# Gated DeltaNet gates with the tokens on the partitions, and an input norm with the token loads first, scaled on VectorE alone

## The chip, the cores and the metric

The kernel runs on one core of one Trainium2 chip. A core has five engines that run side by side and meet only at semaphores: TensorE (PE, matrix products and transposes into PSUM; its weight loads are listed apart as PEld), VectorE (DVE), ScalarE (ACT, activation functions and copies), GpSimd (POOL) and SyncE (SP), which here issues the transfers. Sixteen DMA engines move the data. The metric is the device time of one execution in microseconds, lower is better, given as the median of the runs.

## The reference

One inference step of a two-layer trunk: layer 0 is a gated DeltaNet mixer, layer 1 an RWKV-7 mixer, each behind an RMSNorm and with a residual add. The input is 16 meta tokens and 1024 prompt tokens of one sequence, and 8 sequences of 8 sample tokens with states of their own. The change lies at the start of layer 0:

```
xn = rmsnorm(x, norm_w[0])                      # per token, 1024 features
proj = xn @ w_in                                # qkv (4096), z (2048), b (16), a (16)
qkv = silu(causal_conv(qkv))                    # 4 taps
beta = sigmoid(b)                               # per token and value head
g = -exp(a_log) * softplus(a + dt_bias)         # log decay, per token and value head
gc = cumsum(g) within a chunk
decay = exp(gc[i] - gc[j]), i >= j
A = I + strictly lower (beta k k^T * decay)     # inverted per chunk
```

There are 16 value heads and 8 key heads; value heads 2j and 2j+1 share key head j. Everything behind the gates uses gc in three forms: exp(gc) and exp(gc_last - gc) per token, exp(gc_last) per chunk, and the matrix of differences.

## The kernel before

**Layout.** The 1104 tokens (64 sample tokens, 16 meta tokens, 1024 prompt tokens) are nine tiles of up to 128. Tile 0 holds the 64 sample tokens (eight blocks of 8), the meta tokens and the first 48 prompt tokens. For the products the tokens are the free axis in three segments of 384, 384 and 336, and the features are the partitions. FP32 values are split into a rounded high part and a low rest, and each product of a 128-feature block is three matmuls (high x high, low x high, high x low), so a product of 128 outputs over one segment is 24 matmuls.

**The norm** (`input_norm`, lines 280 to 314) works tile by tile with tokens on the partitions, in the groups {0,1}, {2,3,4}, {5,6}, {7,8}: ACT squares and sums, POOL raises to the power -1/2, DVE refines by a Newton step (lines 111 to 113). Tiles 0, 1, 2, 4, 6 and 8 are then scaled by one DVE instruction (line 299); tiles 3, 5 and 7 are multiplied by the norm weights on POOL (line 291) and scaled on ACT (line 301). PE turns each tile by eight transposes (line 74), ACT copies the high parts (line 309) and DVE subtracts for the low parts (line 313).

**The gates** (`gates_open`, `gates`) have the 16 heads on 16 partitions and all 1104 tokens on the free axis. The product with the 32 gate columns of w_in is `d` with 64 output rows. ACT and DVE work on 16 partitions (lines 361 to 371), one scan makes gc (line 373), and differences to the chunk's last gc are formed by DVE (lines 379 to 382). The decays of the chunks' ends go through memory to all partitions (`dgl` to `eglb`), gc goes to memory as `drow`, and nine transposes turn gates to tokens on partitions, `gcol`, whose four columns are beta, -gc, exp(gc) and exp(gc_last - gc).

**What sets the order.** Up to the first product of layer 0 a planner, which simulates the program, orders every engine. From there on PE and ACT follow a written order: `gdn_events` puts work at slots u, where a slot is half a product over one segment (12 matmuls) and slot -24 is the first half of key head 0's keys. `product` makes the keys (`dk`), queries (`dq`), values (`dv`) and gates (`dz`) of a head in turn; each segment's result is copied by ACT to `raw`, convolved (`cvy`: one tap on ACT, three on DVE, line 524), and passed through SiLU. DVE, POOL and SP still follow the planner.

The gates' stages stand at slots -22.9, -19.4, -16.8, -16.7 and -16.6 (line 928). The pair decays of head 0 (`decays`, line 643: load `E` from `drow`, POOL select, ACT exponentials) are loaded at -18.5, and their exponentials stand from -16 on. Then come the scores (`fsc`, -15.2 to -13.6), the decayed matrix (line 710), its way through memory (`ltd`) to `invA`, and the inversion of 32x32 blocks in 31 steps of two DVE instructions (lines 571 and 573). A transposing copy (line 741) and more transfers (`g_t`, `T1n`) end it, and the first merge of blocks on PE (`rY`, written at slot 2.5) uses it. The attention decays (`attn`) are loaded in the same way; there are three loads of each kind for each of the eight key heads.

Of the kernel before, what the change touches and what calls it, by code (L numbers as in the profile page):

```python
# [11 lines left out]
ALU = mybir.AluOpType  # L12
# [24 lines left out]
class Builder:  # L37
# [242 lines left out]
    def input_norm(self, xh, xl):  # L280
        nc, i, t, lp = self.nc, self.i, self.t, self.lp
        for qs in [[0,1],[2,3,4],[5,6],[7,8]]:
# [3 lines left out]
            for u, q in enumerate(qs):  # L286
                x, nr = self.xrows[q]
                junk = t(lp, [128, D], "junk", 1, BF16)
                self.act(junk[0:nr], x[0:nr], AF.Square, accum=ss[0:nr, u:u + 1])
                if q not in (0,1,2,4,6,8):  # L290
                    nc.gpsimd.tensor_tensor(x[0:nr], x[0:nr], self.nwb[0:nr], op=ALU.mult)
# [3 lines left out]
            for u, q in enumerate(qs):  # L295
                x, nr = self.xrows[q]
                r = rs[0:nr, u:u + 1]
                if q in (0,1,2,4,6,8):
                    nc.vector.scalar_tensor_tensor(x[0:nr], x[0:nr], r, self.nwb[0:nr], op0=ALU.mult, op1=ALU.mult)
                else:  # L300
                    self.act(x[0:nr], x[0:nr], AF.Identity, scale=r)
                c = 128 * q
                for h in (0, 1):
                    p = self.ps("f", 2) if h else self.ps("r", 3)
                    for k in range(4):
                        self.transpose(p[:, 128 * k:128 * k + nr], x[0:nr, 512 * h + 128 * k:512 * h + 128 * k + 128])
# [10 lines left out]
    def gates_open(self, ctx):  # L317
        nc, i = self.nc, self.i
        W = i["gdn_w_in"][0]

        self.col = self.t(self.l0, [128, 9, 4, 16], "gcol")
        self.eglb = self.t(self.l0, [128, 16, 17], "eglb")
        self.bmask4 = self.t(self.l0, [64, 4], "bmask4")
# [3 lines left out]
        t = self.t  # L327
        al = t(gp, [128, 2], "al")
# [5 lines left out]
        rows = t(gp, [96, 1152], "rows")  # L334
        nc.vector.memset(rows, 0.0)
        g = t(gp, [48, 1152], "g")
        nc.vector.memset(g[32:48], 0.0)
        sm = t(gp, [48, 1152], "sm")
        nc.vector.memset(sm[32:48], 1.0)
        nc.gpsimd.memset(sm[32:48].rearrange("p (c k) -> p c k", k=128)[:, :, 0:1], 0.0)  # L340
        nc.gpsimd.memset(sm[32:48, 0:72].rearrange("p (c k) -> p c k", k=8)[:, :, 0:1], 0.0)
        self.gate_in = al, wz, rows, g, sm
        nc.sync.dma_start(al[32:48, 0:1], i["gdn_a_log"].rearrange("l h -> h l"))
        nc.sync.dma_start(al[32:48, 1:2], i["gdn_dt_bias"].rearrange("l h -> h l"))

    def gates(self, xh, xl):
        nc, i, t, gp = self.nc, self.i, self.t, self.gatep
        al, wz, rows, g, sm = self.gate_in
        nea = t(gp, [128, 1], "nea")
        self.act(nea[32:48], al[32:48, 0:1], AF.Exp)  # L350
        nc.vector.tensor_scalar(nea[32:48], nea[32:48], -1.0, None, op0=ALU.mult)
# [4 lines left out]
        x = t(gp, [48, NT], "ax")  # L356
        y = t(gp, [48, NT], "ay")
        for s, (c0, n) in enumerate(SEGS):
            p = self.dense(w, 64, xh, xl, s)
            b = rows[0:16, c0:c0 + n]  # L360
            self.act(b, p[0:16, 0:n], AF.Tanh, scale=0.5)
            nc.vector.tensor_scalar(b, b, 0.5, 0.5, op0=ALU.mult, op1=ALU.add)
            xa, ya = x[32:48, c0:c0 + n], y[32:48, c0:c0 + n]
            self.act(xa, p[32:48, 0:n], AF.Identity, bias=al[32:48, 1:2])
            nc.vector.scalar_tensor_tensor(ya, xa, -1.0, xa, op0=ALU.mult, op1=ALU.max)
            self.act(ya, ya, AF.Exp, scale=-1.0)
        yield
        xa, ya = x[32:48], y[32:48]
        self.act(ya, ya, AF.Ln, bias=1.0)
        nc.vector.scalar_tensor_tensor(ya, xa, 0.0, ya, op0=ALU.max, op1=ALU.add)  # L370
        nc.vector.tensor_scalar(g[32:48, 0:NT], ya, nea[32:48], None, op0=ALU.mult)
        gc = rows[32:48]
        nc.vector.tensor_tensor_scan(gc, sm[32:48], g[32:48], 0.0, op0=ALU.mult, op1=ALU.add)
        yield
        gd = rows[64:80]
        c3 = lambda x: x.rearrange("p (c k) -> p c k", k=128)
        c8 = lambda x: x[:, 0:64].rearrange("p (c k) -> p c k", k=8)
        v, v8 = c3(gc), c8(gc)
        nc.vector.tensor_tensor(c3(gd)[:, 1:9], v[:, 1:9, 127:128].broadcast_to([16, 8, 128]), v[:, 1:9], op=ALU.subtract)
        nc.vector.tensor_tensor(c3(gd)[:, 0:1, 64:128], v[:, 0:1, 127:128].broadcast_to([16, 1, 64]), v[:, 0:1, 64:128],  # L380
                                op=ALU.subtract)
        nc.vector.tensor_tensor(c8(gd), v8[:, :, 7:8].broadcast_to([16, 8, 8]), v8, op=ALU.subtract)
        egl = t(gp, [48, 17], "egl")
        self.act(egl[32:48, 0:8].unsqueeze(2), v8[:, :, 7:8], AF.Exp)
        self.act(egl[32:48, 8:17].unsqueeze(2), v[:, :, 127:128], AF.Exp)
        dgl = self.dram([16, 17], "dgl")
        nc.sync.dma_start(dgl, egl[32:48])
        nc.sync.dma_start(self.eglb.rearrange("p h c -> p (h c)"),
                          dgl.rearrange("(o h) c -> o (h c)", o=1).broadcast_to([128, 272]))

# [530 lines left out]
    def gdn_events(self, G, open_, gate, swap):  # L921
# [6 lines left out]
        for u in (-22.9, -19.4, -16.8, -16.7, -16.6):  # L928
            self.at(u, gate)
# [1622 lines left out]
```

## Time and profile before

| what | value |
|---|---|
| median of 3 runs | 2184.01 us (2181.36 to 2190.6) |
| profiled execution, its own time | 2190.08 us |
| its span on the core | 2188.3 us |
| PE, DVE, ACT, POOL busy | 94%, 72%, 59%, 38% |
| mean granted PE clock | 0.981 |

A busy share is a mean over all stages. In a timeline each row is: start in us, length in us, engine, line, operation, written tile <- read tiles, shapes, how many instructions were merged into the row, and in brackets how long the engine stood before it and what ended that. A row that merges several has their sum as its length. A line can be that of a helper: line 74 is every transpose, line 77 every product, line 63 every activation.

### The profile page before, as it was taken

How to read it: one execution, taken by the hardware profiler on the slowest of the kernel's cores; microseconds unless marked ns; L12 is line 12 of the kernel's file. 1: busy time of each engine (PE TensorE's matmuls, PEld its weight loads, DVE VectorE, ACT ScalarE, POOL GpSimd, SP SyncE). 2: the span in 40 equal slices, each digit the busy share in tenths (PEclk: the TensorE clock that was granted, in tenths of full speed). 3: DMA queues.
4: the chain of work that ended last, by engine and by line, in shares of the span. 5: the costliest groups of instructions: out<-in, count | busy, mean ns of one | idle time of the engine just before them, and what ended most of it. 6: DMA issues, size and time to landing. Idle time of an engine off the chain costs nothing. (4 is left out here: it accounts for less than half of the span.)

```text
span 2188.3 us, 54818 instructions
## 1 busy us (share of the span) xinstructions
PE 2048.3 (94%) x20404; PEld 1905.8 (87%) x20404; DVE 1585.8 (72%) x4221; ACT 1290.9 (59%) x3761; POOL 841.2 (38%) x1125
## 2 busy tenths in 40 slices
PE   5869899999999999999999999999898999999997
PEld 5859899999999999998899999888898988888876
DVE  7967869788887979795334676757968657777755
ACT  5526466656565665656533365664746446777774
POOL 3423333334343333334231352343534344444444
PEclk9979999999999999999999999999999999999999
DMA  4423342424333333335345115655565476677764
GB/s 119 119 58 87 90 115 85 116 78 106 96 96 106 105 96 102 98 102 165 97 126 134 61 51 190 215 167 168 168 180 152 119 221 175 181 229 221 239 178 138
DMA packets 430661, 292.65 MB, mean 134 GB/s; under 512 B 147145, under 2 KB 412986, under 8 KB 430394
## 3 DMA queue, kind: packets, MB, share of 16 engines
q1 hardware_dynamic: 430394, 289.14, 46.0%
q8 instruction: 161, 2.64, 0.5%
q14 instruction: 106, 0.87, 0.1%
HBM read 197.68 MB, written 91.37 MB: 132 GB/s over the span
## 5 line engine op out<-in xcount | busy, mean ns | idle before, releaser
L91 POOL TENSOR_TENSOR wlo<-wraw,whi 128x512 fp32r<-128x512 f32 (+1 forms) x246 | 328.5, 1337 | 475.8 <-ACT whi L87 432.1
L77 PE MATMUL d<-xc,whi 128*128 128x384 f32 (+2 forms) x1006 | 279.1, 336 | 0.8 <-DVE xc L313 0.7
L524 DVE SCALAR_TENSOR_TENSOR cvy<-raw,cw,cvy 128x408 f32<-128x408 f32 (+2 forms) x288 | 189.1, 657 | 19.2 <-ACT cvy L63 17.8
L87 ACT CAST whi<-wraw 128x512 fp32r<-128x512 f32 (+1 forms) x246 | 149.9, 612 | 87.2 <-PE d L77 50.0
L77 PEld LDWEIGHTS d<-xc,whi 128*128 128x128 f32 (+1 forms) x1006 | 183.0, 189 | 3.4 <-DVE xc L313 1.1
L77 PE MATMUL d<-xc,wlo 128*128 128x384 f32 (+3 forms) x476 | 157.5, 339 | 3.8 <-POOL wlo L91 3.8
L77 PE MATMUL dz<-xc,whi 128*128 128x384 f32 (+1 forms) x480 | 153.7, 338 | 0.0
L77 PE MATMUL dv<-xc,whi 128*128 128x384 f32 (+1 forms) x480 | 152.2, 337 | 0.0
L77 PE MATMUL d<-xa,whi 128*128 128x384 f32 (+3 forms) x450 | 142.9, 341 | 8.4 <-ACT ev L2352 4.1
L63 ACT ACTIVATE o<-rA,gcol 128x128 f32<-128x128 f32 x128 | 42.2, 367 | 116.2 <-DVE S L903 116.0
L571 DVE TENSOR_TENSOR invtmp<-invA,invT 72x31 f32<-72x31 f32 (+15 forms) x248 | 101.8, 411 | 3.2
L77 PE MATMUL dv<-xa,whi 128*128 128x384 f32 (+1 forms) x288 | 99.0, 344 | 0.0
L77 PE MATMUL dz<-xa,whi 128*128 128x384 f32 (+1 forms) x288 | 98.5, 342 | 0.0
L77 PEld LDWEIGHTS d<-xc,wlo 128*128 128x128 f32 (+1 forms) x476 | 89.2, 189 | 7.9 <-POOL wlo L91 4.9
L77 PEld LDWEIGHTS d<-xa,whi 128*128 128x128 f32 (+1 forms) x450 | 84.3, 190 | 12.9 <-ACT ev L2352 4.4
L573 DVE TENSOR_TENSOR invT<-invT,invtmp 72x31 f32<-72x31 f32 (+15 forms) x248 | 92.7, 374 | 3.3
L77 PEld LDWEIGHTS dz<-xc,whi 128*128 128x128 f32 x480 | 89.3, 188 | 4.6 <-issue 4.5
L77 PEld LDWEIGHTS dv<-xc,whi 128*128 128x128 f32 x480 | 89.1, 188 | 1.4 <-issue 1.4
L77 PE MATMUL d<-xa,wlo 128*128 128x384 f32 (+3 forms) x252 | 84.8, 337 | 2.0 <-POOL wlo L91 2.0
L77 PE MATMUL dq<-xc,whi 128*128 128x384 f32 (+1 forms) x240 | 78.3, 343 | 3.0 <-ACT whi L87 3.0
L77 PE MATMUL dk<-xc,whi 128*128 128x384 f32 (+1 forms) x240 | 78.2, 346 | 0.0
L1333 DVE SCALAR_TENSOR_TENSOR mixs<-xb,pcol,mixs 128x320 f32<-128x320 f32 (+2 forms) x96 | 69.4, 733 | 5.0 <-ACT mixs L63 4.7
(523 smaller groups left out, 6821.9 us busy)
## 6 DMA issues: line engine op xcount, KB each, us to landing
wraw<-in_gdn_w_in SPq DMA_DIRECT2D x96, 256.0 KB
wraw<-in_rwkv_w_rkvz SPq DMA_DIRECT2D x80, 256.0 KB
Sb<-in_state_gdn SPq DMA_DIRECT2D x64, 256.0 KB
sldcak<-cakd SPq DMA_DIRECT2D x24, 576.0 KB
wraw<-in_rwkv_w_o SPq DMA_DIRECT2D x42, 256.0 KB
E<-drow SPq DMA_DIRECT2D x24, 384.0 KB
attn<-drow SPq DMA_DIRECT2D x24, 384.0 KB
wraw<-in_gdn_w_out SPq DMA_DIRECT2D x36, 256.0 KB
```

Source lines behind the costliest of these rows:

```text
L63: return self.nc.scalar.activation(out, in_, func, bias=bias, scale=scale, **kw)
L77: self.nc.tensor.matmul(out, lhsT, rhs, start=start, stop=stop)
L87: nc.scalar.copy(hi, x)
L91: e.tensor_tensor(lo, x, hi.bitcast(F32), op=ALU.subtract)
L524: nc.vector.scalar_tensor_tensor(y[0][:, 0:wd], raw[:, k:k + wd], cw[k], y[0][:, 0:wd], op0=ALU.mult, op1=ALU.add)
L571: nc.vector.tensor_tensor(tmp, A[:, j, j + 1:32].unsqueeze(2).broadcast_to([nb, n, m]), Tv[:, j, 0:m].unsqueeze(1).broadcast_to([nb, n, m] ...
L573: nc.vector.tensor_tensor(Tv[:, j + 1:32, 0:m], Tv[:, j + 1:32, 0:m], tmp, op=ALU.subtract)
L1333: nc.vector.scalar_tensor_tensor(x[:, f:], xb[:, 8 + a + f:8 + b], mu, x[:, f:], op0=ALU.mult, op1=ALU.add)
```

## The change

**Norm.** All nine tiles are scaled by one DVE instruction; the POOL multiplication and the ACT scaling of tiles 3, 5 and 7 go. The transposes of a tile are issued at high priority for the planner, and the second half of tiles 2, 5 and 8 uses the PSUM bank `m`.

**Loads.** The loads of tiles 3 to 8 are issued ahead of the loads of the gate weights and gate vectors.

**Gates.** The product stays. ACT copies its 48 used rows per segment; nine transposes turn them to tokens on partitions before anything else is done, and everything works on [128, 9, 16]. The scan is replaced by products with four constant 0/1 masks (`upto` for the cumulative sum, `past` for the sum of what follows in the chunk, one of each for tile 0 with its eight short blocks), and the chunks' sums are spread to all partitions by a product with ones instead of through memory. gc is turned back by two transposes and stored as `drow` in the order [tile, head, token], so that a load of two heads and three tiles has three runs per partition instead of one. The stages stand at slots -23.4, -21.4 and -20.4.

```diff
@@ input_norm
-                if q not in (0,1,2,4,6,8):
-                    nc.gpsimd.tensor_tensor(x[0:nr], x[0:nr], self.nwb[0:nr], op=ALU.mult)
...
-                if q in (0,1,2,4,6,8):
-                    nc.vector.scalar_tensor_tensor(x[0:nr], x[0:nr], r, self.nwb[0:nr], op0=ALU.mult, op1=ALU.mult)
-                else:
-                    self.act(x[0:nr], x[0:nr], AF.Identity, scale=r)
+                nc.vector.scalar_tensor_tensor(x[0:nr], x[0:nr], r, self.nwb[0:nr], op0=ALU.mult, op1=ALU.mult)
...
-                    p = self.ps("f", 2) if h else self.ps("r", 3)
-                    for k in range(4):
-                        self.transpose(...)
+                    p = (self.ps("m", 1) if q % 3 == 2 else self.ps("f", 2)) if h else self.ps("r", 3)
+                    with self.tc.high_priority():
+                        for k in range(4):
+                            self.transpose(...)
@@ gates_open
+        for x, nm in enumerate(("gdn_a_log", "gdn_dt_bias")):
+            nc.sync.dma_start(al[:, x], i[nm].broadcast_to([128, 16]))
+        rows = t(gp, [48, 1152], "rows")
+        nc.gpsimd.memset(rows[:, NT:1152], NEG)
+        upto, past = [t(gp, [128, 128], f"upto{k}") for k in (0, 1)], [t(gp, [128, 128], f"past{k}") for k in (0, 1)]
...
@@ gates
+            nc.scalar.copy(rows[:, c0:c0 + n], p[0:48, 0:n])
         yield
+        p = self.ps("f", 2, "gt")
+        for k in range(9):
+            self.transpose(p[:, 48 * k:48 * k + 48], rows[:, 128 * k:128 * k + 128])
+        pv = p[:, 0:432].rearrange("p (k x) -> p k x", x=48)
+        b, x, y, g = [t(gp, [128, 9, 16], n) for n in ("gb", "gx", "gy", "g")]
+        nc.vector.tensor_tensor(x, pv[:, :, 32:48], al[:, 1].unsqueeze(1).broadcast_to([128, 9, 16]), op=ALU.add)
+        nc.vector.scalar_tensor_tensor(y, x, -1.0, x, op0=ALU.mult, op1=ALU.max)
+        self.act(y, y, AF.Exp, scale=-1.0)
+        self.act(b, pv[:, :, 0:16], AF.Tanh, scale=0.5)
+        self.act(y, y, AF.Ln, bias=1.0)
+        nc.vector.scalar_tensor_tensor(y, x, 0.0, y, op0=ALU.max, op1=ALU.add)
+        nc.vector.tensor_tensor(g, y, nea.unsqueeze(1).broadcast_to([128, 9, 16]), op=ALU.mult)
+        gs = t(gp, [128, 9, 16], "gs")
+        nc.vector.tensor_tensor(gs, g[:, 0]..., part..., op=ALU.mult)
+        nc.vector.tensor_scalar(col[:, :, 0, :], b, 0.5, 0.5, op0=ALU.mult, op1=ALU.add)
         yield
+        p = self.ps("f", 2, "gc")
+        for a, m in ((0, upto), (144, past)):
+            self.mm(p[:, a:a + 16], m[0], g[:, 0])
+            self.mm(p[:, a + 16:a + 144], m[1], flat(g[:, 1:9]))
+        c, d = (p[:, a:a + 144].rearrange("p (k h) -> p k h", h=16) for a in (0, 144))
+        nc.vector.tensor_copy(gc, c)
+        e = self.ps("m", 1, "ge")
+        self.mm(e[:, 0:144], self.ones, flat(gs))
+        self.mm(e[:, 144:272], self.ones, flat(g[:, 1:9]))
+        self.act(col[:, :, 1, :], c, AF.Identity, scale=-1.0)
+        self.act(self.eglb.rearrange("p h c -> p c h"), e[:, 0:272]..., AF.Exp)
+        self.act(col[:, :, 2, :], c, AF.Exp)
+        self.act(col[:, :, 3, :], d, AF.Exp)
+        yield
+        p = self.ps("f", 2, "gr")
+        self.transpose(p[:, 0:128], flat(gc[:, 0:8]))
+        self.transpose(p[0:16, 128:256], gc[:, 8])
+        nc.vector.tensor_copy(r[:, 0:128], p[:, 0:128])
+        nc.vector.tensor_copy(r[0:16, 128:256], p[0:16, 128:256])
+        self.drow = self.dram([9, 16, 128], "drow")
+        nc.sync.dma_start(self.drow[0:8].rearrange("t h k -> (t h) k"), r[:, 0:128])
+        nc.sync.dma_start(self.drow[8], r[0:16, 128:256])
@@ decays
-                          self.drow[j, 3 * s:3 * s + 3].rearrange("(o t) h k -> o (t h k)", o=1).broadcast_to([128, 768]))
+                          self.drow[3 * s:3 * s + 3, 2 * j:2 * j + 2].rearrange("(o t) h k -> o t (h k)", o=1).broadcast_to([128, 3, 256]))
@@ gdn_events
-        for u in (-22.9, -19.4, -16.8, -16.7, -16.6):
+        for u in (-23.4, -21.4, -20.4):
             self.at(u, gate)
@@ layer0
+        self.input_load(range(3, 9))
         self.gates_open(gates)
-        self.input_load(range(3, 9))
         self.input_norm(hi, lo)
```

98 lines of the change are left out of this document (31 added, 67 removed).

## The prediction

> **What bounds the kernel now.** I read, in this order: the head of the profile page, busy time by stage, the TensorE (PE) timeline of the first 145 us, and the timelines of the engines that PE waits for there.
>
> The page's head, then the view of busy time by stage (columns: stage, its length, busy us and count of PE, PEld, DVE, ACT, POOL, then PE clock, DMA share, GB/s):
>
> ```profile
> span 2188.3 us, 54818 instructions
> ```
>
> ```profile
> 12.17:45.59 33.42, 23.21 (x137) 18.92 (x138) 30.70 (x54) 23.94 (x45) 16.70 (x16) 1.00 0.39 126
> 45.59:73.40 27.81, 23.59 (x129) 22.05 (x128) 17.46 (x33) 12.76 (x29) 7.25 (x17) 0.88 0.26 68
> 73.40:137.10 63.70, 45.25 (x329) 42.80 (x327) 61.86 (x171) 26.96 (x76) 23.87 (x35) 0.91 0.31 85
> ```
>
> The profiled execution took 2190.08 us, 1.8 us round its span. In the norm (12.17 to 45.59) DVE is busy 30.7 of 33.4 us and PE 23.2; from 73.4 to 137.1 DVE is busy 61.9 of 63.7 us and PE only 45.3. In both stages DVE is the bound; between them it has 10 us to spare and waits for PE. Now PE's timeline (start, us, engine, line, operation, tiles, shapes, count, idle before it and who ended it):
>
> ```profile
> 26.82 0.42 PE L77 MATMUL d<-xa,whi 128*64 128x384 f32 x1
> ...
> 44.83 0.42 PE L77 MATMUL dk<-xa,whi 128*128 128x384 f32 x1
> ...
> 64.99 0.69 PE L77 MATMUL dq<-xc,whi 128*128 128x384 f32 x1 [3.02 <-ACT whi L87]
> 66.42 0.69 PE L77 MATMUL dq<-xc,wlo 128*128 128x384 f32 x1 [0.74 <-POOL wlo L91]
> ...
> 69.79 0.52 PE L77 MATMUL dq<-xc,whi 128*128 128x384 f32 x1
> 70.11 1.05 PE L74 MATMUL f<-ident,rows 96*128 96x96 f32 x6
> 72.12 0.34 PE L77 MATMUL dq<-xa,wlo 128*128 128x384 f32 x1
> 72.29 0.34 PE L77 MATMUL dq<-xc,whi 128*128 128x384 f32 x1
> 74.04 0.83 PE L77 MATMUL fsc<-K 128*128 128x128 f32 x6
> ...
> 141.32 0.31 PE L77 MATMUL rY<-T1n,E 32*32 32x32 f32 x2 [20.04 <-DMA T1n<-g_t]
> ```
>
> PE's written order reaches the first merge of key head 0 at 121.3 and stands 20.04 us, because the inverse isn't there. So the instant of that merge, not PE's work before it, sets when everything behind it starts. The DVE timeline shows what the merge waits for:
>
> ```profile
> 60.10 2.55 DVE L373 TENSOR_TENSOR_SCAN rows<-sm,g 16x1152 f32<-16x1152 f32 x1
> ...
> 73.40 0.66 DVE L524 SCALAR_TENSOR_TENSOR cvy<-raw,cw,cvy 128x408 f32<-128x408 f32 x1 [0.96 <-ACT cvy L63]
> ...
> 89.15 1.64 DVE L710 SCALAR_TENSOR_TENSOR E<-fsc,bp,E 128x128 f32<-128x128 f32 x6
> ...
> 97.65 0.17 DVE L571 TENSOR_TENSOR invtmp<-invA,invT 72x31 f32<-72x31 f32 x1
> ...
> 136.08 1.02 DVE L741 COPY invA<-invT 72x1024 f32<-72x1024 f32 x1
> ```
>
> DVE begins an almost unbroken run at 73.40, with the first convolution tap of the queries; the inverse runs in it from 97.65 and ends at 136.08. 5.2 us of transfers later the merge starts. The change helps by as much as it moves the 73.40.
>
> **The change part by part.** The norm first: DVE's timeline, two groups of DVE in 12 to 46 us (count | busy us, mean ns | idle before), POOL's timeline:
>
> ```profile
> 12.17 0.16 DVE L111 TENSOR_TENSOR rn_t<-rs 128x2 f32<-128x2 f32 x1 [0.90 <-POOL rs L103]
> 19.71 2.30 DVE L111 TENSOR_TENSOR rn_t<-rs 128x3 f32<-128x3 f32 x1 [0.33 <-POOL rs L103]
> 27.07 2.35 DVE L111 TENSOR_TENSOR rn_t<-rs 128x2 f32<-128x2 f32 x1 [0.22 <-POOL rs L103]
> 37.50 1.27 DVE L299 SCALAR_TENSOR_TENSOR x<-x,rs,nwb 80x1024 f32<-80x1024 f32 x1
> ```
>
> ```profile
> L362 DVE TENSOR_SCALAR rows<-rows 16x384 f32<-16x384 f32 x2 | 1.3, 636 | 0.0
> L365 DVE SCALAR_TENSOR_TENSOR ay<-ax 16x384 f32<-16x384 f32 x2 | 1.1, 548 | 0.1
> ```
>
> ```profile
> 19.64 2.35 POOL L291 TENSOR_TENSOR x<-x,nwb 128x1024 f32<-128x1024 f32 x1
> ...
> 27.00 2.40 POOL L291 TENSOR_TENSOR x<-x,nwb 128x1024 f32<-128x1024 f32 x1
> ```
>
> Three more tiles are scaled on DVE: 3 x 1.27 = +3.8. The gates' L362 and L365 leave this stage: -2.4. Three POOL multiplications go. Two of them start just before a DVE instruction of two or three columns does, which then takes 2.30 and 2.35 where the same instruction takes 0.16 at 12.17: -4.3 if that time is simply freed, 0 if other POOL work takes their place. The three ACT scalings that go lie beside DVE, and so do some 16 more small constants on POOL, which is busy half of this stage (16.7 of 33.4); if POOL weren't free, they'd hold up the powers that DVE's L111 waits for. Sum on DVE: -2.9, with bounds of +1.4 and, if the two DVE idles of the stage (33.4 - 30.7 = 2.7) close as well, -5.6. I take **-2.9**.
>
> The Trainium skill (SBUF — State Buffer, "Who interferes with whom") says that a DVE instruction with two SBUF inputs and a GpSimd instruction that reads SBUF exclude each other for a whole instruction. The two rows of 2.3 agree. By that rule the 4.3 are freed in full, but each added scaling has two SBUF inputs and can itself stand behind a POOL split; by it I would expect the sum nearer -2 than -2.9.
>
> Earlier token loads I price at nothing (SP's queue):
>
> ```profile
> 6.45 4.45 SPq L343 DMA_DIRECT2D al<-in_gdn_a_log  x1
> 11.40 2.83 SPq L264 DMA_DIRECT2D x<-in_x_prompt  x6
> ```
>
> Six tiles stop queueing behind 4.45 us of gate vectors, so they come some 5 us sooner, but DVE's queue of work covers that: it is 92% busy. Without that cover they'd be worth the 2.7 us of idle above. The gate weights now land behind them; their product started at 26.82, far behind.
>
> From the keys' first product to the end of the queries' first third (44.83 to 70.11) PE loses 3.02 + 0.74 in stalls, both behind ACT's written order, which stood for the convolution behind DVE's 16-partition gate work (scan 2.55 and its neighbours). That stall also drops the pace: 0.32 us from the matmul at 69.79 to the next instruction against 0.17 at 72.12; the 11 from 66.42 to 70.11 took 3.7 instead of 1.9. Sum **-5.5**. PE gains work in the same stretch: nine transposes of 48 rows (six of 96 columns took 1.05 at the slow pace, so about 0.9 for nine of half the width at the full one), a wait for the last copy of rows (ACT: 0.44 and a hand-over, 0.6), six cumulative products (three of 128x128 took 0.83: at most 1.7) and two transposes (0.3): **+3.5**. The old nine transposes lay behind 70.11, so their going helps only what comes later. Net -2.0.
>
> Here is ACT's part of it:
>
> ```profile
> 50.49 0.44 ACT L63 ACTIVATE rows<-d 16x336 f32<-16x336 f32 x1 [4.94 <-PE d L77]
> 53.08 1.28 ACT L63 ACT_TABLE_LOAD   x1
> 54.38 1.22 ACT L63 ACTIVATE ay<-ay,cvals 16x1104 f32<-16x1104 f32 x1
> 63.89 0.54 ACT L63 ACTIVATE raw<-cvy 128x408 f32<-128x408 f32 x1 [4.74 <-DVE cvy L524]
> 71.25 0.67 ACT L63 ACTIVATE gcol<-f 128x48 f32<-128x48 f32 x4 [0.36 <-PE f L74]
> 72.73 0.64 ACT L63 ACTIVATE cvy<-raw,cw 128x408 f32<-128x408 f32 x1
> ```
>
> The gate column exponentials stand between the queries' copy and their first tap; they go, so the tap follows the copy about 1 us after PE's end instead of 2.6: **-1.6**. The new gate chain (add, absolute value, exp, tanh, table load, ln, three products on 144 columns) is about 0.6 + 0.7 + 1.3 + 0.4 + 0.9 = 3.9 us from these rows' sizes, against a cover of two written slots of 12 matmuls, 4.1. If the cover were missing, PE would stand those 3.9. What queues behind: on ACT the copies of the keys, on PE the keys' second third.
>
> The Trainium skill (ScalarE: Activation LUTs, "What ACT_TABLE_LOAD costs") adds 1.38 us of drain to each 1.28 us load. Here the activation starts 0.02 us after the load, so no drain is seen in this row; by the page the chain would be 5.3 us, PE would wait 1.2, and the sum would be 1.2 smaller.
>
> Sum: -2.9 - 2.0 - 1.6 = -6.5. From the 73.40 on, DVE's 62 us of work holds no gate instruction, and its order of kind stays; PE's own head start at the queries (2.9 + 2.0, and about 1.75 for the old transposes behind 70.11) is as large as DVE's, so PE will again wait 20 us or so for the merge, without harm. The inverse ends near 129.6, the merge starts near 134.8. Behind it PE is busy and shifts as a whole. 2190.1 - 6.5 = 2183.6 against its own execution; against the median of 2184.0 it is **2177.5**.
>
> The pair and attention rows now load as three runs of 1 KB per partition instead of one of 3 KB. No row has that, so: 0, bounded below by 0 (more pieces of the same bytes can't be quicker) and above by the last rival. On SP two stores of the cumulative rows replace eight, and the two transfers of the last decays go; SP waits for nothing of it but the pair loads, which are issued three slots later, so 0.
>
> **The rivals.** *A, the inverse moves more.* Its 62 steps need 11.5 + 10.4 us by themselves:
>
> ```profile
> L571 DVE TENSOR_TENSOR invtmp<-invA,invT 72x31 f32<-72x31 f32 (+15 forms) x31 | 11.5, 369 | 0.7
> L573 DVE TENSOR_TENSOR invT<-invT,invtmp 72x31 f32<-72x31 f32 (+15 forms) x31 | 10.4, 336 | 0.7
> ```
>
> It took 38.4 (97.65 to 136.08), so 16.5 us of other work was mixed in. DVE's order comes from a planner's simulation; if half of that falls behind the inverse, 8 us more are won: 2169. For it: PE waits long enough. Against: the same planner mixed them before.
>
> *B, nothing moves.* If the planner, seeing gates earlier, puts the first inverse step ahead of convolution work, DVE stands until its matrix has made its way through memory, which in this run lies between the last L710 (ends at 90.8) and 97.65: up to 6.9 us, which eats the 6.5: 2184. Against: in the run up to 97.65 there's hardly idle time.
>
> *C, slower.* The rearranged pair loads take longer. An attention load, its select and its exponentials (SP, POOL, ACT):
>
> ```profile
> 1035.10 0.38 SPq L647 DMA_DIRECT2D attn<-drow  x1
> 1039.96 0.87 POOL L651 TENSOR_SCALAR_AFFINE_SELECT attn<-attn 128x768 f32<-128x768 f32 x1 [0.46 <-DMA attn<-drow]
> 1041.74 1.95 ACT L63 ACTIVATE attn<-attn,gcol 128x128 f32<-128x128 f32 x6
> ```
>
> It lands 4.9 us after its issue and has 0.9 us of slack until ACT, whose order is written, wants it. There are 24. Each us beyond 0.9 delays ACT and the PE evacuations behind it: with loads 1.5 us longer, 24 x 0.6 = 14.4 - 6.5 = +8, 2192. It is slower than before once a load takes 1.2 us more. For it: three times the pieces. Against: the bytes are the same.
>
> **How the numbers follow.** Forecast 0.48, A 0.24, B 0.15, C 0.13. The forecast's own range is the sum of its bounds: norm -5.6 to +1.4, PE's additions 3.5 to 6, so 2174 to 2184. Less than 0.5% (10.9 us) can't be told from no change here. Faster than that (below 2173): five sixths of A and three tenths of the forecast, 0.34; slower (above 2195): half of C and what the rest leaves, 0.11; within: 0.55. Range 2163 to 2193: A's full price (16.5 more would be 2161) nearly to its end, C's middle at the other.
>
> **What would show it.** Right: the DVE run that ends in the inverse's transposing copy starts near 67, ends near 130; the rY wait is again about 20 us and ends near 135; no PE stall of 3 us between 55 and 70; L111 never over 1 us in the norm; the norm's last residual near 42.7. Wrong: a wait of several us at the cumulative products (the chain outran its cover), DVE idle ahead of the first L571 (B), POOL's waits on attn far above one load (C), or a merge near 141 with all that in order.

## The result and the profile after

The changed kernel takes **2301.14 us** (median of 4 runs, 2296.42 to 2305.88) beside 2184.31 of the kernel before: ratio 1.0531, 95% interval 1.0495 to 1.0567. It is 117 us slower; forecast were 2177.5 us, a range up to 2193, and a chance of 0.11 for slower.

The profiled execution took 2297.26 us. The heads of the two pages (busy us, share of the span, instructions; then PE's busy share in 40 slices), first before:

```profile
PE 2048.3 (94%) x20404; PEld 1905.8 (87%) x20404; DVE 1585.8 (72%) x4221; ACT 1290.9 (59%) x3761; POOL 841.2 (38%) x1125
...
PE   5869899999999999999999999999898999999997
```

Then after:

```profile
span 2295.5 us, 54812 instructions
...
PE 2084.4 (91%) x20418; PEld 1934.3 (84%) x20418; DVE 1555.2 (68%) x4212; ACT 1284.4 (56%) x3750; POOL 816.3 (36%) x1136
...
PE   6769899798898989989999999989999999999997
```

Of the 107 us between the two profiled spans (2295.5, 2188.3), 71 are idle time of PE (211 us, 140 before) and 36 are the same matmuls at a slower granted clock (0.963, 0.981 before). The slices show where: from 150 to 1150 us, the whole gated DeltaNet stage, with eights among the nines. The first four slices hardly differ (6769 after, 5869 before). Busy time by stage in the middle of that stage, before:

```profile
300.00:500.00 200.00, 196.78 (x1612) 189.06 (x1613) 169.34 (x491) 123.10 (x409) 73.58 (x106) 1.00 0.37 102
```

and after (same columns as in the prediction):

```profile
300.00:500.00 200.00, 176.91 (x1363) 167.88 (x1362) 134.74 (x408) 108.73 (x361) 58.73 (x89) 0.94 0.41 88
```

PE has lost 20 of 200 us. And the transfer engines are *more* busy (0.41 beside 0.37) while they move *less* (88 beside 102 GB/s): something holds them without moving bytes. The view of waits (waiting engine, line, released by; us in total, times, longest) points at the pair loads, before:

```profile
POOL attn L651 <- DMA attn<-drow: 55.3, 17, 7.1
POOL E L651 <- DMA E<-drow: 8.6, 5, 3.4
...
PE rY L77 <- DMA T1n<-g_t: 27.6, 5, 20.0
PE rA L77 <- DVE S L903: 2.8, 7, 0.7
```

and after:

```profile
POOL attn L652 <- DMA attn<-drow: 89.2, 15, 11.2
POOL E L652 <- DMA E<-drow: 68.6, 17, 7.0
...
PE rY L77 <- DMA T1n<-g_t: 37.1, 12, 20.1
PE dz L77 <- POOL wlo L91: 32.9, 5, 7.6
PE rA L77 <- DVE S L904: 25.9, 20, 3.1
PE dv L77 <- POOL wlo L91: 12.7, 2, 11.6
```

By these rows GpSimd stands 94 us more at the selects of the pair loads. PE has four waits that are new or longer: two for weight splits of GpSimd (dz and dv on wlo), one for the state S of the chunk recurrence, and one for the inverse's transfers. The transfer packets in the two traces fit that: the E and attention loads were 6144 packets of 3 KB and are 18432 of 1 KB. A load lasts 2.1 us (median) before and 5.6 us after, which is 70 GB/s for its 393,216 bytes (84 in the quickest, 4.7 us). Over the first load and the start of the second (59.4 to 65 us) the rate stays near its mean of 83 GB/s while the engines' busy share goes from 0.2 to 0.9.

At the start the gates come early, and what they win is lost at the first load. SP's and POOL's timelines, after:

```profile
57.89 1.43 SPq L648 DMA_DIRECT2D E<-drow  x3
...
75.60 0.86 POOL L652 TENSOR_SCALAR_AFFINE_SELECT E<-E 128x768 f32<-128x768 f32 x1 [4.58 <-DMA E<-drow]
```

Before, the three loads were issued at 67.06 and the last select ran at 73.88. Now they are issued 9.2 us sooner, and the last select runs 1.7 us later, at 75.60. The inverse's transposing copy stands at 140.88 instead of 136.08.

### The profile page after: what moved, and what is told of

Same layout as the page of the kernel before. It is cut to its first block, busy times and chain, and to the rows that moved or that the text cites. A ratio compares the mean times of both kernels' runs of the same rounds, so it can differ in the third digit from the quotient of the medians.

```text
span 2295.5 us, 54812 instructions
## 1 busy us (share of the span) xinstructions
PE 2084.4 (91%) x20418; PEld 1934.3 (84%) x20418; DVE 1555.2 (68%) x4212; ACT 1284.4 (56%) x3750; POOL 816.3 (36%) x1136
## 5 line engine op out<-in xcount | busy, mean ns | idle before, releaser
L77 PE MATMUL dz<-xc,whi 128*128 128x384 f32 (+1 forms) x480 | 159.3, 350 | 0.0
L77 PE MATMUL dz<-xc,wlo 128*128 128x384 f32 (+1 forms) x192 | 67.5, 352 | 32.9 <-POOL wlo L91 32.9
L77 PEld LDWEIGHTS d<-xc,wlo 128*128 128x128 f32 (+1 forms) x476 | 88.9, 188 | 6.9 <-POOL wlo L91 3.8
L77 PE MATMUL rA<-S,K 128*128 128x128 f32 x256 | 50.0, 297 | 36.1 <-DVE S L904 25.9
```

What stands on the lines that cost most here:

```text
L77: self.nc.tensor.matmul(out, lhsT, rhs, start=start, stop=stop)
```

## The experiments

**Are the loads the whole loss?** The theory: only the three-run loads are slow, and all else does what the sum said. The rival: masks, products or the norm's new order cost something of their own. First the changed kernel with the old layout:

```diff
+        gq = t(gp, [128, 8, 8, 2], "gq")
+        nc.vector.tensor_copy(gq, gc[:, 0:8].rearrange("p t (j e) -> p j t e", e=2))
...
-        self.drow = self.dram([9, 16, 128], "drow")
-        nc.sync.dma_start(self.drow[0:8].rearrange("t h k -> (t h) k"), r[:, 0:128])
-        nc.sync.dma_start(self.drow[8], r[0:16, 128:256])
+        self.drow = self.dram([8, 9, 2, 128], "drow")
+        for j in range(8):
+            nc.sync.dma_start(self.drow[j, 0:8].rearrange("t h k -> (t h) k"), r[16 * j:16 * j + 16, 0:128])
+        for h in (0, 1):
+            nc.sync.dma_start(self.drow[:, 8, h], r[8 * h:8 * h + 8, 128:256])
@@ decays: one run of 768, as before
```

> The changed kernel with the cumulative rows stored as before, [key head, tile, head, token], and the pair loads in one run of 3 KB; two VectorE copies turn the heads before the transposes, and ten stores replace two. The order of PE, DVE and ACT stays that of the changed kernel but for these instructions. If the three-run loads are the whole loss: 2170 to 2182, the prediction's sum without its last part (2177.5). If the gates or the norm cost something of their own: above 2195. If the loads are not the cause: 2290 to 2305.

Measured: 2172.58 us (4 runs) beside 2181.78, ratio 0.9957 (0.994 to 0.9974). The rest of the change makes the kernel 9.4 us faster (5.7 to 13.1), against 6.5 in the sum. Its DVE timeline, to be read beside that of the prediction:

```profile
65.26 1.35 DVE L531 SCALAR_TENSOR_TENSOR cvy<-raw,cw,cvy 128x408 f32<-128x408 f32 x1 [0.95 <-ACT cvy L63]
...
67.72 3.61 DVE L531 SCALAR_TENSOR_TENSOR cvy<-raw,cw,cvy 128x408 f32<-128x408 f32 x1
...
91.54 0.18 DVE L578 TENSOR_TENSOR invtmp<-invA,invT 72x31 f32<-72x31 f32 x1
...
129.97 1.02 DVE L748 COPY invA<-invT 72x1024 f32<-72x1024 f32 x1
```

and PE's:

```profile
135.21 0.31 PE L77 MATMUL rY<-T1n,E 32*32 32x32 f32 x2 [20.06 <-DMA T1n<-g_t]
```

Inverse and merge come 6.1 us sooner than before (136.08 to 129.97, 141.32 to 135.21), and PE's wait is 20.06 as it was 20.04. DVE's run itself begins 8.1 us sooner (73.40 to 65.26); 2.0 of them are lost before the inverse's first step (91.54, 97.65 before).

Then the other way about: the kernel before, with nothing but the new layout and the three-run loads.

```diff
-        self.drow = self.dram([8, 9, 2, 128], "drow")
-        for j in range(8):
-            nc.sync.dma_start(self.drow[j].rearrange("t h k -> h t k"), c3(gc)[2 * j:2 * j + 2])
+        self.drow = self.dram([9, 16, 128], "drow")
+        for j in range(8):
+            nc.sync.dma_start(self.drow[:, 2 * j:2 * j + 2].rearrange("t h k -> h t k"), c3(gc)[2 * j:2 * j + 2])
@@ decays: three runs of 256, as in the change
```

> The kernel before with the new layout of the cumulative rows and the three-run loads alone, nothing else of the change. If the loads are the whole loss: 2290 to 2315 (2184 + 117 + the 6.5 that the rest was expected to win). If the loss needs the rest of the change, for instance the gates' earlier slots: below 2200.

Measured: 2300.2 us in one run, 118 us above the 2181.78 of the kernel before. The loads in the new layout are the whole loss, with the old gates as with the new.

**Why is the load slow?** Loads one at a time behind the end of the kernel before, each followed by one small DVE read:

```diff
+        def runs(n, k, pitch):
+            v = x[0:n * pitch].rearrange("(o t k) -> o t k", o=1, t=n)[:, :, 0:k]
+            return v.broadcast_to([128, n, k])
...
+                for _ in range(times):
+                    E = self.t(pool, [128, *shape], tag)
+                    for d, s in srcs:
+                        nc.sync.dma_start(d(E), s)
+                    nc.vector.tensor_copy(j[:, 0:1], E[:, 0, 0:1])
```

> The kernel before, with loads appended behind its end, one at a time: each load fills 128 partitions and is followed by one small VectorE read; the next load waits for that. Four of each form; 'b' forms give all partitions the same bytes, 'd' forms give each partition its own. In the trace of the changed kernel a load in three runs of 1 KB, 8 KB apart, takes 5.6 us where one run of 3 KB took 2.1. Pieces: a piece of 1 KB is dear in itself; then every form with 384 pieces of 1 KB takes some 3.5 us more than the 3 KB form, the 'd' form with 1 KB pieces too, and six pieces of 512 B take longer still (over 9 us). Engines: three runs are shared out to three or four DMA engines only; then every form of three runs is slow whatever its pitch, 'd' too, six runs take about half as long, and three separate loads of 1 KB are as fast as one of 3 KB. Pitch: runs 8 KB apart fall on the same part of memory; then 1.5 KB and 12 KB apart are as fast as 3 KB, 8 KB apart is slow. Same place: 16 engines read the same 1 KB at once and one place in memory gives about 84 GB/s; then all 'b' forms in 1 KB pieces are slow, three separate loads too, a single load of 1 KB takes 1.6 us for its bytes (131 KB), and the 'd' form is as fast as 3 KB.

DVE's timeline, the form of 3 KB and the form of the change (start of the read; its idle time is the wait for the load; two loads' reads lie one load apart):

```profile
2229.66 0.15 DVE L2148 COPY seen<-b3k 128x1 f32<-128x1 f32 x1 [3.29 <-DMA b3k<-in_x_prompt]
...
2240.15 0.15 DVE L2148 COPY seen<-b1kx3p8k 128x1 f32<-128x1 f32 x1 [6.34 <-DMA b1kx3p8k<-in_x_prompt]
2247.16 0.15 DVE L2148 COPY seen<-b1kx3p8k 128x1 f32<-128x1 f32 x1 [6.86 <-DMA b1kx3p8k<-in_x_prompt]
...
2369.32 0.15 DVE L2148 COPY seen<-d1kx 128x1 f32<-128x1 f32 x1 [3.09 <-DMA d1kx<-in_x_prompt]
```

All forms, from read to read (means of the three intervals of a form; the first interval of the separate loads was shortened by an early issue and is left out):

| load of 128 partitions | us |
|---|---|
| same bytes to all: one run of 3 KB | 3.6 |
| same bytes: 3 x 1 KB, 8 KB apart (the change) | 6.9 |
| same bytes: 3 x 1 KB, 1.5 KB apart | 3.8 |
| same bytes: 3 x 1 KB, 8.5 KB / 12 KB apart | 5.1 / 5.1 |
| same bytes: three separate loads of 1 KB, 8 KB apart | 6.6 |
| same bytes: 6 x 512 B, 4 KB apart | 7.3 |
| same bytes: 2 x 1.5 KB, 8 KB apart | 5.1 |
| same bytes: one run of 1 KB (a third of the bytes) | 3.3 |
| each partition its own: 3 x 1 KB | 3.3 |
| each partition its own: one run of 3 KB | 3.1 |

"Pieces" falls: 384 pieces of 1 KB from places of their own take 3.3 us. "Engines" falls with it: that load has the same three runs. (The Trainium skill, "DMA: Bandwidth & Descriptors", section "Why a DMA increments its semaphore by 16 and not by 1", lets the slowest dimension choose the number of engines; here it is the 128 partitions, so by it all sixteen work, and the trace agrees: 3.3 us beside 3.1 for one run of 3 KB from places of its own.) "Pitch" and "same place" are each half right: the distance decides, but 12 KB is no cure. What fits all nine forms of the same bytes, within 0.7 us, is a **fold**: addresses 8 KB apart count as one place, and a place of 512 bytes yields about 42 GB/s; 2 us come on top. By that, pieces at 0, 8 and 16 KB share two such places (393 KB over 84 GB/s, 4.7 + 2), and pieces at 0, 12 and 24 KB share them two and one (3.1 + 2).

A fit found afterwards proves little, so it had to forecast other distances, and a cure:

```diff
+            for nm, k in (("p1k", 256), ("p2k", 512), ("p3k", 768), ("p4k", 1024), ("p6k", 1536), ("p9k", 2304), ("p10k", 2560), ("p16k", 4096), ("p8k", 2048), ("p8k25", 2112)):
+                form(nm, (3, 256), [(all_, runs(3, 256, k))])
```

> Again the kernel before with loads behind its end, all filling 128 partitions with the same three pieces of 1 KB, only their distance in memory differs. The eleven forms of the first such run fit a fold: memory counts as the same place every 8 KB, each 512 bytes of the fold give about 42 GB/s, and 2 us come on top; the time is set by the place that has most to give. By the fold (from one VectorE read to the next): 1, 2, 3, 6, 9 and 10 KB apart 3.5 to 3.9 us, 4 KB apart 5.1 (pieces 1 and 3 share a place), 8 and 16 KB apart 6.6 to 7.1, 8.25 KB apart about 6.6. By distance alone (pieces more than 4 KB apart are slow, whatever the fold): 6, 9 and 10 KB apart take over 5 us too. By a need for a pitch of several KB more than the power of two: 9 and 10 KB apart are no better than 8.5 KB was, 5.1. Then pairs: a load of 3 KB per partition at places of its own, queued right behind a broadcast one. If transfers of a queue are served in turn, it lands some 3.3 us later behind pieces 8 KB apart than behind pieces side by side.

| distance of the 1 KB pieces, KB | fold says, us | measured, us |
|---|---|---|
| 1, 2, 3 | 3.5 to 3.9 | 3.6, 4.0, 3.8 |
| 4 | 5.1 | 5.1 |
| 6 | 3.5 to 3.9 | 3.8 |
| 9, 10 | 3.5 to 3.9 | 3.8, 4.0 |
| 8, 16 | 6.6 to 7.1 | 6.9, 6.4 |
| 8.25 | 6.6 | 6.7 |

The fold holds within 0.2 us at every distance. "By distance alone" falls (6, 9 and 10 KB are fast), and so does the need for a pad of several KB (9 KB is fast). The Trainium skill ("DMA: Bandwidth & Descriptors", section "Latency and other measured facts") knows slow row pitches at large powers of two, from 2 MiB up and with 512 KiB still at near full rate, and advises a pad of a few KB. Here a distance of 8 KB is enough when all partitions read the same bytes (6.9 us); 1 KB of padding cures it (3.8), and 4 KB cure half of it (5.1). The pairs of loads in this run told nothing, since the second loads were issued ahead of the first.

**The cure in the kernel:** room for 18 heads instead of 16, so that tiles lie 9 KB apart.

```diff
-        self.drow = self.dram([9, 16, 128], "drow")
-        nc.sync.dma_start(self.drow[0:8].rearrange("t h k -> (t h) k"), r[:, 0:128])
-        nc.sync.dma_start(self.drow[8], r[0:16, 128:256])
+        self.drow = self.dram([9, 18, 128], "drow")
+        for k in range(8):
+            nc.sync.dma_start(self.drow[k, 0:16], r[16 * k:16 * k + 16, 0:128])
+        nc.sync.dma_start(self.drow[8, 0:16], r[0:16, 128:256])
```

> The changed kernel, loads in three runs of 1 KB as there, but the rows of a tile stored with room for 18 heads in place of 16, so that the three runs lie 9 KB apart and not 8; nine stores replace two. By the fold, the loads are as fast as one run of 3 KB: 2168 to 2178, like the old layout's 2172.6, perhaps 1 us less since two VectorE copies go. By distance alone: 2240 to 2305.

Measured: 2179.56 us (10 runs) beside 2186.36, ratio 0.9973 (0.9955 to 0.999); the inverse's copy stands at 129.57. That is a little above the 2168 to 2178 expected, beside a kernel before that also measured 4.6 us more than in the old layout's comparison. Same pieces, same loads, same order of PE, DVE and ACT as the changed kernel, 1 KB of distance (and nine stores instead of two): 122 us (1.0531 less 0.9973, of 2184). The old layout and this one can't be told apart in time; both beat the kernel before and the changed one.

**The parts of the gain.** The norm alone, and the gates alone with the old layout:

> The kernel before with the changed norm, the turns at high priority and the token loads first; gates, layout and loads as before. The prediction's sum gave the norm -2.9 of -6.5 and the stall behind the old gates' chain stays: 2177 to 2182 beside a before of 2182. If the norm carries nearly all: below 2175.

> The kernel before with the changed gates, the cumulative rows stored in the old layout and loaded in one run; norm and load order as before. The prediction's sum gave this part -3.6 of -6.5: 2176 to 2181 beside a before of 2182. If the gates' masks and constants on POOL hold up the old norm's POOL multiplications: 2182 or more.

```diff
@@ r8: before, with input_norm of the change and
+        self.input_load(range(3, 9))
         self.gates_open(gates)
-        self.input_load(range(3, 9))
@@ r9: the old-layout kernel above, with input_norm and the order of the loads of before
```

Measured: norm alone 2187.53 us (10 runs) beside 2186.36, ratio 1.0003 (0.9986 to 1.002): nothing, where 0 to 5 us had been expected. Gates alone 2179.21 (10 runs), 0.9966 (0.9951 to 0.9982): 7.4 us faster, where 1 to 6 had been expected; the interval, 3.9 to 10.7, reaches into that. PE's timeline with the norm alone, with the stalls that the prediction quoted as 3.02 and 0.74:

```profile
40.74 0.34 PE L77 MATMUL dk<-xa,whi 128*128 128x384 f32 x1
...
62.47 0.44 PE L77 MATMUL dq<-xc,whi 128*128 128x384 f32 x1 [3.93 <-ACT whi L87]
64.28 0.69 PE L77 MATMUL dq<-xc,wlo 128*128 128x384 f32 x1 [1.38 <-POOL wlo L91]
```

and DVE's:

```profile
97.24 0.19 DVE L567 TENSOR_TENSOR invtmp<-invA,invT 72x31 f32<-72x31 f32 x1 [0.79 <-DMA invA<-ltd]
135.70 1.03 DVE L737 COPY invA<-invT 72x1024 f32<-72x1024 f32 x1
```

The keys start 4.1 us sooner (40.74, 44.83 before). The stalls behind the old gates grow by 1.6 us, DVE then stands 0.79 us for the inverse's matrix, and 0.4 us is left at the inverse's end. With the gates alone that end is at 132.18, 3.9 us sooner; with both, 6.1. So at the inverse the norm's part is worth 2.2 us once the gates' chain is out of the way, and 0.4 before. In the whole time that isn't seen: 2179.21 us with the gates alone, 2179.56 with both and rows 9 KB apart, measured side by side.

**How do 48 loads, 3.4 us longer each, cost 120 us?** Rival C priced the attention loads by their slack. Two versions of the 9 KB kernel, each with a second copy of the rows 8 KB apart, from which one kind of load reads:

```diff
-                          self.drow[3 * s:3 * s + 3, 2 * j:2 * j + 2]...
+                          (self.drow8 if tag == "attn" else self.drow)[3 * s:3 * s + 3, 2 * j:2 * j + 2]...
@@ the other run: if tag == "E"
```

> The changed kernel with rows 9 KB apart, and a second copy of the rows 8 KB apart, from which the attention decays alone are loaded (24 slow loads); the pair decays E load fast. Rival C of the prediction, with the size that the loads alone showed (3.4 us more in place of 1.5): 24 x (3.4 - 0.9) = 60 us over the version with all loads fast, so about 2235 to 2245, and nothing left for E but what makes the 120 full. If the loss goes by loads, whichever tile they fill: the same 60. If it came from E alone: below 2190.

> The other way about: E alone is loaded from rows 8 KB apart, the attention decays fast. If only the attention loads have too little slack, as rival C had it: below 2190. If the loss goes by loads: some 60 us over the fast version, 2235 to 2245. The two runs' losses should add up to the 120 of the changed kernel; if the sum is far less, the slow loads hurt by following one another.

Measured beside 2186.77: attention loads slow 2241.06 us (2 runs), ratio 1.0245 (1.0209 to 1.028); E slow 2236.83 (2 runs), 1.0226 (1.0191 to 1.026). Against the 0.9973 of the 9 KB kernel that is 59 and 55 us, together 115 of the 122. PE's waits tell the two apart; attention loads slow:

```profile
PE rY L77 <- DMA T1n<-g_t: 36.3, 13, 20.1
PE rA L77 <- DVE S L908: 24.9, 21, 2.8
...
DVE on_t L111 <- POOL ors L103: 79.6, 22, 6.3
...
ACT attn L63 <- POOL attn L656: 4.4, 1, 4.4
```

and E slow:

```profile
PE dz L77 <- POOL wlo L91: 31.4, 5, 7.2
PE rY L77 <- DMA T1n<-g_t: 27.7, 6, 20.1
PE dv L77 <- POOL wlo L91: 8.9, 2, 5.2
PE rA L77 <- DVE S L908: 3.5, 7, 1.1
...
DVE on_t L111 <- POOL ors L103: 23.8, 17, 3.8
```

The four waits of the changed kernel fall apart almost cleanly (with attention loads slow, one wait of 4.3 us for dv is left). Both kinds of load do their harm through GpSimd's queue. With the attention loads slow, what is late behind their selects is `ors`, the power -1/2 of the output norm: VectorE stands 79.6 us for it, 23.4 in the 9 KB kernel, and VectorE's next work is the state S, for which PE waits. POOL's rows at one such place, then DVE's and PE's:

```profile
457.19 0.87 POOL L656 TENSOR_SCALAR_AFFINE_SELECT attn<-attn 128x768 f32<-128x768 f32 x1 [10.87 <-DMA attn<-drow]
...
459.26 1.32 POOL L103 TENSOR_TENSOR ors<-ovar,cvals 128x6 f32<-128x6 f32 x1
...
460.62 0.17 DVE L111 TENSOR_TENSOR on_t<-ors 128x6 f32<-128x6 f32 x1 [5.90 <-POOL ors L103]
...
461.51 0.49 PE L77 MATMUL rA<-S,K 128*128 128x128 f32 x2 [2.76 <-DVE S L908]
```

ScalarE, which rival C had waiting for the attention decays, waits for such a select once in the whole run (4.4 us; 1.4 in the 9 KB kernel). The chain by way of `ors` is read from the trace; no run took that power off GpSimd. With E slow, the weight splits are what is late. POOL's timeline there, one head:

```profile
411.99 1.21 POOL L656 TENSOR_SCALAR_AFFINE_SELECT E<-E 128x768 f32<-128x768 f32 x1 [5.62 <-PE rU L77]
...
417.25 1.00 POOL L656 TENSOR_SCALAR_AFFINE_SELECT E<-E 128x768 f32<-128x768 f32 x1 [3.30 <-issue]
...
421.81 0.86 POOL L656 TENSOR_SCALAR_AFFINE_SELECT E<-E 128x768 f32<-128x768 f32 x1 [2.64 <-issue]
...
422.68 1.26 POOL L91 TENSOR_TENSOR wlo<-wraw,whi 128x512 fp32r<-128x512 f32 x1
```

and PE's:

```profile
424.00 0.69 PE L77 MATMUL dz<-xc,wlo 128*128 128x384 f32 x1 [5.76 <-POOL wlo L91]
```

Three selects stand 11.6 us for their loads, the split for dz follows at 422.68, and PE has waited 5.76 us for it. (The rows don't name the loads, but the loads' last packets ended 1.6, 0.7 and 0.3 us before the three selects began; where rows of this run name the load, that gap is 0.4 to 1.8.) With fast loads the same three selects stand 3.5 us.

**Late by themselves, or what stands behind them?** Two tries. First an idle transfer of the slow shape behind each fast load, to memory nobody reads:

```diff
+        nc.sync.dma_start(self.idle, self.i["x_prompt"][0].rearrange("a b -> (a b)")[0:6144].rearrange("(o t k) -> o t k", o=1, t=3)[:, :, 0:256].broadcast_to([128, 3, 256]))
```

> The changed kernel with rows 9 KB apart, all pair loads fast, and behind each of the 48 an idle transfer of the same shape as the slow load (128 times the same three pieces of 1 KB, 8 KB apart) to a place in memory that nobody reads. Nobody waits for it, it only holds the transfer engines some 4.7 us. If the loss comes from what is queued behind the slow loads (weights, states, the inverse's transfers): most of the 120 us comes back, over 2250. If it comes from the pair loads' own late landing, with GpSimd standing at their selects and its queue behind: below 2200.

Measured: 2415.64 us (ratio 1.1043, 1.0986 to 1.11), but it doesn't answer the question. Nothing tied the idle transfers to their loads, and all 48 were issued by 413.9 us. They write the same place, so each waited on SP for the one before, 280 us in all, with everything else on that queue behind it; PE's longest stall there was 88.9 us, and it ran at 196 of 200 us afterwards. Then the pair loads on GpSimd's own queue, slow and fast:

```diff
-        nc.sync.dma_start(E.rearrange("p t h k -> p t (h k)"),
+        nc.gpsimd.dma_start(E.rearrange("p t h k -> p t (h k)"),
```

> The changed kernel (rows 8 KB apart, slow loads), but the 48 pair loads are issued by GpSimd on a queue of their own, so that weights, states and the inverse's transfers on SP's queue need not stand behind them. To be read against the same with rows 9 KB apart. If the 120 us come from what stands behind the slow loads in the queue: less than 40 us between the two. If they come from the pair loads' own late landing, GpSimd standing at the selects: 80 us or more between the two.

> Rows 9 KB apart (fast loads), the 48 pair loads issued by GpSimd on a queue of their own: the control for the run above. GpSimd is busy 38% of the time, so the issues themselves should cost little: 2175 to 2215, however long one takes there.

Measured: slow 2285.83 us (1.0459, 1.0429 to 1.0489), fast 2194.97 (1.0034, 1.0013 to 1.0055): 91 us between them, where it was 122 on SP's queue. By the expectation that speaks for the loads' own lateness. But the runs also show that a queue of its own doesn't free the inverse's transfers. The store g_t is issued by SP, and the loads T1n behind it wait for it to land. With fast pair loads on GpSimd's queue the two issues lie 3.7 to 4.1 us apart from the third key head on:

```profile
612.47 0.30 SPq L746 DMA_DIRECT2D g_t<-invT  x1
616.13 1.53 SPq L749 DMA_DIRECT2D T1n<-g_t  x3
```

With the rows 8 KB apart, the loads on GpSimd's queue too, 5.4 to 7.1 us, no less than in the changed kernel, where all is on SP's queue (5.1 to 6.3):

```profile
669.50 0.30 SPq L745 DMA_DIRECT2D g_t<-invT  x1
674.91 1.40 SPq L748 DMA_DIRECT2D T1n<-g_t  x3
```

The Trainium skill ("DMA: Bandwidth & Descriptors", section "Issuing engines are not separate DMA queues") says that transfers run on the same 16 engines whoever issues them; these rows agree. The last run asked whether a transfer behind a slow one on the same queue waits at all:

```diff
+                    nc.sync.dma_start(E[:, 0:3], first)
+                    nc.sync.dma_start(E[:, 3], x[0:32768].rearrange("(p k) -> p k", p=128))
+                    nc.vector.tensor_copy(j[:, 1:2], E[:, 3, 0:1])
+                    nc.vector.tensor_copy(j[:, 0:1], E[:, 0, 0:1])
```

> The kernel before with pairs of loads behind its end: a broadcast load in three pieces (side by side; 9 KB apart; 8 KB apart), and right behind it on the same queue a load of 1 KB per partition from places of its own. VectorE reads the second first, then the first. If the queue serves in turn, the second lands together with the first or a little behind it, so 3 us later behind the pieces 8 KB apart; if the second can pass, its read starts as early in all three cases.

It waits. The two reads ran the other way about: line 2155 reads the slow load first, line 2154 then the one behind it. The pieces lie 8 KB apart:

```profile
2268.25 0.15 DVE L2155 COPY seen<-far 128x1 f32<-128x1 f32 x1 [6.80 <-DMA far<-in_x_prompt]
2268.63 0.15 DVE L2154 COPY seen<-far 128x1 f32<-128x1 f32 x1 [0.22 <-DMA far<-in_x_prompt]
```

Line 2154 still stands 0.22 us for its own load when the first read is done, so the second load landed behind the slow one. From pair to pair it is 7.3 us; with pieces 9 KB apart 4.4, and there too the second lands behind the first in two of the four pairs. So both ways are real. How the 120 us divide between them stays open: some 30 of them went with the shared queue, if the two comparisons can be subtracted so, and the other 91 hold both the selects that stand and the transfer engines that are held.

## Why the prediction was wrong, and where it was right

**What bounds the kernel** held. The early bound moved as argued: the inverse and its merge in the kernel with fast loads stand 6.1 us sooner, forecast 6.5; the merge waited 20.06 us again and started at 135.21, forecast 134.8; the inverse's copy stands at 129.97, forecast 129.6. How close that is, is partly luck. DVE's run was to start near 67 and started at 65.26, 1.6 us earlier than the sum said; on the way to the inverse's first step 2.0 us were lost again. The one row shown at 67.72 accounts for more than that: a convolution tap that takes 0.63 us at 66.96 takes 3.61 there, beside selects and a weight split of GpSimd from 67.94 to 70.88 (before, the longest such tap of the run took 1.72).

**The step that failed** is the last of the sum: "The pair and attention rows now load as three runs of 1 KB per partition instead of one of 3 KB. No row has that, so: 0". It measured +122 us. The lower bound, 0, had an argument; the point taken was that lower bound, and the upper bound was a rival at 0.13 whose price stopped at 2192. What the runs show in place of the 0: 3.4 us more for each of 48 loads, because their three pieces lie 8 KB apart, and GpSimd standing at the selects with splits and powers for PE and VectorE queued behind.

**Rival C** had the right cause, slower loads, with the wrong size and the wrong waiter. It took 1.5 us more per load; a load took 3.4 more. It priced 24 attention loads only; the 24 E loads, which have no term in it, cost 55, as their selects stand in GpSimd's queue ahead of the weight splits. And it had each attention load delay ScalarE past a slack of 0.9 us, which was read at one load. Its formula with the measured size, 24 x (3.4 - 0.9) = 60, comes out at what the attention loads cost when they alone are slow (59), but the traces don't show that path: ScalarE waits for one select, and the wait that grows is VectorE's for `ors` behind the selects on GpSimd (23.4 to 79.6 us). Of the 53.6 us between the profiled spans of that run and the 9 KB kernel, 36 are idle time of PE and 17 the same matmuls at a slower clock (0.975, 0.979), for which the formula has no term. So that agreement is luck. "Against: the bytes are the same" was the argument that misled. The bytes were the same; the addresses were not, and the new tensor's row of 16 heads x 128 tokens x 4 bytes is 8192 bytes.

**The parts.** The norm: its last residual ended at 45.59 before and ends at 41.20 in the old-layout kernel, 4.4 us sooner, forecast 2.9, within the bounds. No row of L111 there is over 0.17 us, as forecast, but the lock with POOL went to other small instructions:

```profile
24.81 1.11 DVE L355 TENSOR_SCALAR nea<-nea 128x16 f32<-128x16 f32 x1
...
25.91 1.26 DVE L290 TENSOR_SCALAR ss<-ss 128x2 f32<-128x2 f32 x1
```

Each ends just as a weight split of POOL does (24.60 to 27.15, two of them), and each would take some 0.16 alone, so 2 us of the 4.3 came back. (In the changed kernel itself one L111 row has 1.31.) The Trainium skill's section weighed in the prediction (SBUF — State Buffer, "Who interferes with whom") also names `tensor_scalar`, in the two-port modes, among those that can exclude GpSimd; these rows (1.11 and 1.26 us) agree. But the sum's parts were added as if each were worth its own length, and they aren't: the norm alone measures 0 and moves the inverse by 0.4, because the gates' stall takes it back. PE's stalls of 3.02 and 0.74 went, as forecast, and the new gate chain cost PE one wait of 0.44, forecast 0.6; its cover of two slots held, and the drain that would have made PE wait 1.2 isn't seen here either (in the old-layout kernel ACT's table load starts at 48.86, 0.02 us behind the activation before it, takes 1.28, and the next activation starts at 50.16).

**Small slips that cost nothing here:** the pair loads stand 1.9 slots behind the last gates' stage, not three, and the chances put three tenths of the forecast below 2173, where its own range starts at 2174.

**Rivals A and B:** the inverse, from its first step to its copy, took 38.4 to 38.7 us in every one of these kernels, so A didn't happen. B's stall for the inverse's matrix shows only with the norm alone, at 0.79 us.

**What should have warned:** two rows of the trace before. GpSimd already stood 17 times for an attention load and 5 times for E (55.3 and 8.6 us), with work for PE and VectorE behind it in its queue, so an unknown price on that load could be paid up to 48 times. A cost without a row, with such a factor, deserved a range, not a 0.

## What to carry to other kernels

When an edit changes how a buffer in memory is laid out, write down the distance in bytes between the pieces that one load reads: for a load that gives all partitions the same bytes, three pieces of 1 KB took 6.4 to 6.9 us at 8 and 16 KB apart and 3.6 to 4.0 at most other distances, and a pad of 1 KB cured it. A transfer with little slack that is issued for every head must be priced with its count, and with what stands behind its waiter in that engine's queue. And a saving ahead of a stall can be taken back by it: with the norm alone the keys started 4.1 us sooner and the inverse 0.4, while the old gates' stall stood.

## What was not expected of the hardware

- Reads by all partitions of the same 1 KB pieces, 8 or 16 KB apart, ran at about 84 GB/s (6.4 to 6.9 us for 384 KB, of which the fit takes 2 us as fixed); at 1, 2, 3, 6, 9 or 10 KB apart they took 3.6 to 4.0, and at 4 KB 5.1. That memory folds every 8 KB fits all 19 broadcast forms tried, nine of them afterwards (within 0.7 us) and ten as forecast (within 0.2, the distance of 8 KB among them again); what in the memory does so was not looked into.
- With the slow loads the transfer engines show as busier (0.41 of their time from 300 to 500 us, 0.37 before) at fewer GB/s (88, 102).
- A store on SP's queue was later by 1.7 us and more when slow loads ran on GpSimd's queue (from the third key head on 5.4 to 7.1 us to the load that waits for it, 3.7 to 4.1 beside loads of rows 9 KB apart).
- A convolution tap on VectorE that takes 0.63 us took 3.61 while GpSimd ran selects and a split (old-layout kernel, 67.72).
